# Cross-covariance attention on one core: every hand-off between engines one unit later

## The chip, the cores and the metric

The kernel runs on one core of one Trainium2 chip. The metric is the device time of one execution in microseconds. TensorE (PE) multiplies, VectorE (DVE) and ScalarE (ACT) work on elements, GpSimd (POOL) computes one small power here, and SyncE (SP) issues all transfers. Each engine takes its instructions strictly in the order in which they were written, and semaphores make it wait for the others. "PEld" in the profile is the loading of TensorE's weights.

## The reference

Q, K and V are 8 x 12 x 512 x 64 in float32: 96 heads of 512 rows and 64 columns. The attention is between columns, not rows.

```python
Q_norm = Q / (np.linalg.norm(Q, axis=-2, keepdims=True) + 1e-10)
K_norm = K / (np.linalg.norm(K, axis=-2, keepdims=True) + 1e-10)
attn = np.einsum('bhnd,bhne->bhde', Q_norm, K_norm)
attn = np.exp(attn - np.max(attn, axis=-1, keepdims=True))
attn = attn / (np.sum(attn, axis=-1, keepdims=True) + 1e-10)
return np.einsum('bhnd,bhde->bhne', V, attn).astype(np.float32)
```

## The kernel before

The 96 heads are worked in 24 units (U = 24) of four heads. For one unit the steps are, with the names that stand in the code and in the profile:

- **load_qk, load_v** (SyncE, L72, L73, L77): Q, K and V of the unit, 0.524 MB each, into buffers qf, kf, vf. Each has five buffers, so the load of unit u waits until unit u−5 has been cast.
- **casts** (VectorE, L85 to L88): Q and K of each head side by side in bf16, qkb. Before, the same function also casts V to vb (L90).
- **grams** (TensorE, L98): 16 matmuls of qkb with itself, so that one product holds QᵀQ, QᵀK and KᵀK (gram, two buffers in PSUM).
- **norms** (VectorE, L106): four masked sums over the diagonals of gram give the squared column norms nsq; GpSimd raises them to the power −0.5 (rq, L111).
- **scale_k** (VectorE, L117): the QᵀK blocks times the norms of K, kqs. It is the last reader of gram.
- **logits** (TensorE, L125): turns kqs into place, lg (one buffer in PSUM).
- **exps** (ScalarE, L131): exp with the norm of Q as its scale and the row sum beside it.
- **normalise** (VectorE, L137, L140): division by the sum, at in bf16.
- **doubled** (TensorE L146, then two ScalarE copies, L148 and L149): two copies of at, dup, then spread over a block-diagonal buffer ab (three of them, used in turn).
- **vtrans** (TensorE L156, then a ScalarE copy L158): eight transposes of vb, vps, then vt.
- **outs** (TensorE L168, then two ScalarE copies L172): V times the attention, 32 small matmuls, po, then so in float32 (ten buffers).
- **store** (SyncE, L80): 0.524 MB of output.

Nothing reorders these instructions: the order on each engine is that of the program text, in the loop over the steps s. In step s, the kernel before works on grams, norms, vtrans and scale_k of unit s, on logits, exps, normalise and doubled of unit s−1, on outs of unit s−2 and the casts of unit s+1. SyncE's queue holds, in this order, the loads of unit s+3 and the store of unit s−6, and is as strictly in order as the engines. Waits follow from the buffers: a step that writes a buffer waits until the last reader of its former content is done.

Of the kernel before, what the change touches and what calls it, by code (L numbers as in the profile page):

```python
# [25 lines left out]
def kernel(  # L26
# [11 lines left out]
    U = BH // HU  # L38
# [22 lines left out]
    ps_o = ctx.enter_context(tc.tile_pool(name="ps_o", bufs=2, space=bass.MemoryType.PSUM))  # L61

    LOAD_AHEAD = 3
    CAST_AHEAD = 1
    STORE_LAG = 6

# [2 lines left out]
    def load_qk(u):  # L69
        qf[u] = qp.tile([128, HU, T, D], F32, name="qf")  # L70
        kf[u] = qp.tile([128, HU, T, D], F32, name="kf")
        nc.sync.dma_start(out=qf[u], in_=Qf[:, u * HU:(u + 1) * HU])  # L72
        nc.sync.dma_start(out=kf[u], in_=Kf[:, u * HU:(u + 1) * HU])  # L73

    def load_v(u):
        vf[u] = vp.tile([128, SV, RV * D], F32, name="vf")
        nc.sync.dma_start(out=vf[u], in_=Vf[:, u * SV:(u + 1) * SV])  # L77

    def store(u):
        nc.sync.dma_start(out=Of[:, u * SV:(u + 1) * SV], in_=so[u])  # L80

    def casts(u):

        t_ = qkb[u] = qkp.tile([128, HU, T, 2 * D], BF16, name="qkb")
        nc.vector.tensor_copy(t_[:, 0::2, :, 0:D], qf[u][:, 0::2])  # L85
        nc.vector.tensor_copy(t_[:, 1::2, :, D:2 * D], qf[u][:, 1::2])  # L86
        nc.vector.tensor_copy(t_[:, 0::2, :, D:2 * D], kf[u][:, 0::2])  # L87
        nc.vector.tensor_copy(t_[:, 1::2, :, 0:D], kf[u][:, 1::2])  # L88
        w = vb[u] = vbp.tile([128, SV, TP, 2 * D], BF16, name="vb")
        nc.vector.tensor_copy(w.rearrange("p s t d -> p s (t d)"), vf[u])  # L90

    def grams(u):
        g = gram[u] = ps_g.tile([128, PU, 4, D], F32, name="gram")
        for h in range(HU):
            o = g[:, h // 2, 2 * (h % 2):2 * (h % 2) + 2, :]
            for t in range(T):
                x = qkb[u][:, h, t, :]
                nc.tensor.matmul(o, x, x, start=(t == 0), stop=(t == T - 1))  # L98

    def norms(u):  # L100

        n2 = nsq[u] = small.tile([128, 2, PU], F32, name="nsq")
        for p in range(PU):
            for c, (blk, m) in enumerate(((gram[u][:, p, 0::3, :], mask_q), (gram[u][:, p, 1:3, :], mask_k))):
                scr = small.tile([128, 2, D], F32, name="scr")
                nc.vector.tensor_tensor_reduce(  # L106
                    out=scr, in0=blk, in1=m, scale=1.0, scalar=1e-20,
                    op0=ALU.mult, op1=ALU.add, accum_out=n2[:, c, p:p + 1],
                )
        r = rq[u] = small.tile([128, 2, PU], F32, name="rq")  # L110
        nc.gpsimd.tensor_tensor(out=r, in0=n2, in1=mhalf, op=ALU.pow)  # L111

    def scale_k(u):

        kk = kqs[u] = small.tile([128, PU, 2, D], F32, name="kqs")
        for p in range(PU):
            nc.vector.scalar_tensor_tensor(  # L117
                out=kk[:, p], in0=gram[u][:, p, 0::3, :], scalar=rq[u][:, 1, p:p + 1], in1=off_diag,
                op0=ALU.mult, op1=ALU.mult,
            )  # L120

    def logits(u):
        l = lg[u] = ps_l.tile([128, PU, D], F32, name="lg")
        for p in range(PU):
            nc.tensor.matmul(l[:, p, :], kqs[u][:, p].rearrange("p a d -> p (a d)"), eye2)  # L125

    def exps(u):
        e = ex[u] = small.tile([128, PU, D], F32, name="ex")
        s = small.tile([128, PU], F32, name="esum")
        for p in range(PU):  # L130
            nc.scalar.activation(e[:, p, :], lg[u][:, p, :], AF.Exp, scale=rq[u][:, 0, p:p + 1], accum_out=s[:, p:p + 1])  # L131
        ex[u] = (e, s)

    def normalise(u):
        e, s = ex[u]
        ri = small.tile([128, PU], F32, name="rinv")
        nc.vector.reciprocal(ri, s)  # L137
        a = at[u] = small.tile([128, PU, D], BF16, name="at")
        for p in range(PU):
            nc.vector.tensor_scalar_mul(a[:, p, :], e[:, p, :], ri[:, p:p + 1])  # L140

    def doubled(u):

        d = ps_d.tile([128, 2, PU, D], F32, name="dup")
        for c in range(2):
            nc.tensor.matmul(d[:, c], pick[:, c, :], at[u])  # L146
        a = ab[u] = abuf[u % len(abuf)]
        nc.scalar.copy(a[0:D, :, :, 0, :], d[0:D].rearrange("p c u d -> p u c d"))  # L148
        nc.scalar.copy(a[D:, :, :, 1, :], d[D:].rearrange("p c u d -> p u c d"))  # L149

    def vtrans(u):

        ps = ps_v.tile([128, SV, TP, 128], BF16, name="vps")
        for g in range(SV):
            for t in range(TP):
                nc.tensor.transpose(ps[:, g, t, :], vb[u][:, g, t, :], identb)  # L156
        w = vt[u] = vtp.tile([128, SV, TP, 128], BF16, name="vt")
        nc.scalar.copy(w, ps)  # L158

    def outs(u):  # L160
        s = so[u] = sop.tile([128, SV, TP, 2 * D], F32, name="so")
        for i in range(2):
            po = ps_o.tile([128, 4, 2 * D], F32, name="po")
            for k in range(4):
                g, t = divmod(4 * i + k, TP)
                for x in range(HS):
                    h = g * HS + x
                    nc.tensor.matmul(  # L168
                        po[NV * x:NV * (x + 1), k, :], vt[u][:, g, t, NV * x:NV * (x + 1)],
                        ab[u][:, h // 2, h % 2].rearrange("p a d -> p (a d)"), tile_position=(0, NV * x),  # L170
                    )
            nc.scalar.copy(s.rearrange("p g t d -> p (g t) d")[:, 4 * i:4 * i + 4, :], po)  # L172


    for u in range(LOAD_AHEAD):
        load_qk(u)
        load_v(u)

    ident = const.tile([128, 128], F32, name="ident")
    make_identity(nc, ident)  # L180
# [24 lines left out]

    for u in range(CAST_AHEAD):
        casts(u)
    for s in range(U + 2):
        if s + LOAD_AHEAD < U:
            load_qk(s + LOAD_AHEAD)  # L210
            load_v(s + LOAD_AHEAD)
        if 0 <= s - STORE_LAG:
            store(s - STORE_LAG)
        if 0 <= s - 1 < U:
            logits(s - 1)
            exps(s - 1)
        if s < U:
            grams(s)
            norms(s)
            vtrans(s)  # L220
        if s + CAST_AHEAD < U:
            casts(s + CAST_AHEAD)
        if 0 <= s - 1 < U:
            normalise(s - 1)
        if s < U:
            scale_k(s)
        if 0 <= s - 2 < U:
            outs(s - 2)
        if 0 <= s - 1 < U:
            doubled(s - 1)  # L230
    for u in range(U + 2 - STORE_LAG, U):
        store(u)


# [28 lines left out]
```

## Time and profile before

| | us |
|---|---|
| median of 3 runs (167.81 to 170.22) | 169.07 |
| the profiled execution | 170.53 |
| its span, first to last instruction | 168.4 |
| PE busy | 105.2 (62%) |
| DVE busy | 94.6 (56%) |
| ACT busy | 83.4 (50%) |
| POOL busy | 33.7 (20%) |

The granted TensorE clock was 0.742 of full speed on average. In the groups and timelines of the profile a line gives the engine, the operation, what it writes and reads ("gram<-qkb"), the count, the busy time and the mean of one; in brackets or behind a bar stand the idle time ahead of it and what ended it. The chain of work is followed back from the last instruction. Buffer numbers are left out in the profile.

### The profile page before, as it was taken

To read this page: it belongs to the slowest core of one execution; us is meant where nothing else is said; L and a number is where in the kernel's file an instruction comes from. 1 tells how busy PE (TensorE), PEld (TensorE's weight loads), DVE (VectorE), ACT (ScalarE), POOL (GpSimd) and SP (SyncE) were. 2 spreads that over 40 slices of the span, in tenths; PEclk is the share of its full clock that TensorE was granted. 3 is DMA by queue.
4 is the path that set the end of the run, shared out by engine and by line. 5 is a ranking of instruction groups with operands and counts; after the bars stand their busy time and mean duration, and the time that the engine had idled before them with its cause. 6 is when DMAs were issued, how large, how long until landed. Compare 5 with 4: busy or idle time off the path is not lost.

```text
span 168.4 us, 4020 instructions
## 1 busy us (share of the span) xinstructions
PE 105.2 (62%) x1488; PEld 92.0 (55%) x1488; DVE 94.6 (56%) x432; ACT 83.4 (50%) x217; POOL 33.7 (20%) x45
## 2 busy tenths in 40 slices
PE   0427376494595667495595558486496687696860
PEld 0317275394484456385494457376385476495740
DVE  0573844836746863935845963844945853935410
ACT  3021354446437473546447483645555644446561
POOL 8220320302202220211202220220220220311200
PEclk9999996968769696967858796967858555555555
DMA  5999999999999999999999999999999303023053
GB/s 181 300 381 367 367 366 367 366 366 367 380 392 385 395 396 390 389 392 396 374 354 362 301 343 376 377 305 345 309 294 410 131 33 128 30 96 128 0 242 131
DMA packets 32274, 50.58 MB, mean 300 GB/s; under 512 B 1536, under 2 KB 26112, under 8 KB 32256
## 3 DMA queue, kind: packets, MB, share of 16 engines
q1 hardware_dynamic: 32256, 50.34, 85.2%
q8 instruction: 11, 0.18, 0.4%
q14 instruction: 7, 0.06, 0.1%
HBM read 37.75 MB, written 12.58 MB: 299 GB/s over the span
## 4 chain that ended last, share of the span: by engine, by line
DVE 46%; PE 40%; DMA 6%; issue 3%; SPq 1%; ACT 1%; POOLq 1%; ACTq 0%; DVEq 0%
PE gram L98 22%; PE lg L125 13%; DVE scr L106 12%; DVE vb L90 8%; DVE at L140 6%; DMA vf<-in_V_dram 6%; DVE qkb L85 4%; PE dup L146 4%; DVE qkb L87 4%; DVE qkb L88 4%; DVE qkb L86 4%; DVE rinv L137 1%; POOLq L258 1%; SPq L73 1%; SPq L72 1%
## 5 line engine op out<-in xcount | busy, mean ns | idle before, releaser
L111 POOL TENSOR_TENSOR rq<-nsq,mhalf 128x4 f32<-128x4 f32 x24 | 29.4, 1226 | 124.3 <-DVE nsq L106 118.8
L158 ACT COPY vt<-vps 128x1024 bf16<-128x1024 bf16 x24 | 24.3, 1012 | 46.1 <-PE vps L156 46.1
L98 PE MATMUL gram<-qkb 128*128 128x128 bf16 x384 | 43.1, 301 | 6.2 <-DVE qkb L87 6.2
L106 DVE CUSTOM_DVE_ANT_0 scr<-gram,ident 128x128 f32<-128x128 f32 x48 | 13.9, 289 | 56.3 <-PE gram L98 56.3
L98 PEld LDWEIGHTS <-qkb 128*128 128x128 bf16 x384 | 41.1, 148 | 6.2 <-DVE qkb L87 6.2
L146 PE MATMUL dup<-at,pick 128*128 128x128 bf16 x48 | 7.8, 253 | 45.7 <-DVE at L140 45.7
L146 PEld LDWEIGHTS <-pick 128*128 128x128 bf16 x48 | 3.0, 102 | 50.5 <-DVE at L140 47.7
L172 ACT COPY so<-po 128x512 f32<-128x512 f32 x48 | 25.9, 598 | 0.7 <-PE po L168 0.7
L125 PE MATMUL lg<-eye,kqs 128*128 128x64 f32 x96 | 22.6, 381 | 5.0 <-DVE kqs L117 4.1
L156 PE MATMUL vps<-identb,vb 128*128 128x128 bf16 x192 | 23.4, 297 | 1.1 <-DVE vb L90 1.1
L125 PEld LDWEIGHTS lg<-eye,kqs 128*128 128x128 f32 x96 | 19.0, 278 | 9.1 <-issue 4.5
L156 PEld LDWEIGHTS <-vb 128*128 128x128 bf16 x192 | 20.1, 144 | 1.4 <-DVE vb L90 1.4
L148 ACT CAST ab<-dup 64x256 bf16<-64x256 f32 x24 | 8.8, 366 | 24.3 <-PE dup L146 24.3
L168 PE MATMUL po<-ab,vt 128*32 128x128 bf16 x768 | 19.6, 261 | 0.9 <-ACT ab L149 0.9
L131 ACT ACTIVATE ex<-lg,rq 128x64 f32<-128x64 f32 x48 | 14.6, 309 | 9.2 <-PE lg L125 8.8
L90 DVE CAST vb<-vf 128x1024 bf16<-128x1024 f32 x24 | 16.4, 684 | 2.6 <-DMA vf<-in_V_dram 2.6
L168 PEld LDWEIGHTS <-vt 128*32 128x32 bf16 x768 | 14.6, 117 | 4.7 <-issue 3.6
L117 DVE SCALAR_TENSOR_TENSOR kqs<-gram,rq,off_diag 128x128 f32<-128x128 f32 x48 | 14.5, 344 | 0.7 <-POOL rq L111 0.7
L106 DVE CUSTOM_DVE_ANT_0 scr<-gram,swap 128x128 f32<-128x128 f32 x48 | 13.7, 286 | 0.0
L85 DVE CAST qkb<-qf 128x512 bf16<-128x512 f32 x24 | 10.8, 452 | 4.2 <-DMA qf<-in_Q_dram 4.2
L140 DVE TENSOR_SCALAR at<-ex,rinv 128x64 bf16<-128x64 f32 x48 | 10.0, 252 | 0.8
L87 DVE CAST qkb<-kf 128x512 bf16<-128x512 f32 x24 | 10.0, 418 | 0.7 <-DMA kf<-in_K_dram 0.7
(23 smaller groups left out, 56.1 us busy)
## 6 DMA issues: line engine op xcount, KB each, us to landing
qf<-in_Q_dram SPq DMA_DIRECT2D x24, 512.0 KB, 9.4
kf<-in_K_dram SPq DMA_DIRECT2D x24, 512.0 KB, 10.3
vf<-in_V_dram SPq DMA_DIRECT2D x24, 512.0 KB, 10.2
out_dram<-so SPq DMA_DIRECT2D x24, 512.0 KB, 8.3
```

What stands on the lines that cost most here:

```text
L85: nc.vector.tensor_copy(t_[:, 0::2, :, 0:D], qf[u][:, 0::2])
L90: nc.vector.tensor_copy(w.rearrange("p s t d -> p s (t d)"), vf[u])
L98: nc.tensor.matmul(o, x, x, start=(t == 0), stop=(t == T - 1))
L106: nc.vector.tensor_tensor_reduce(out=scr, in0=blk, in1=m, scale=1.0, scalar=1e-20, op0=ALU.mult, op1=ALU.add, accum_out=n2[:, c, p:p + 1],)
L111: nc.gpsimd.tensor_tensor(out=r, in0=n2, in1=mhalf, op=ALU.pow)
L125: nc.tensor.matmul(l[:, p, :], kqs[u][:, p].rearrange("p a d -> p (a d)"), eye2)
L140: nc.vector.tensor_scalar_mul(a[:, p, :], e[:, p, :], ri[:, p:p + 1])
L146: nc.tensor.matmul(d[:, c], pick[:, c, :], at[u])
L156: nc.tensor.transpose(ps[:, g, t, :], vb[u][:, g, t, :], identb)
L158: nc.scalar.copy(w, ps)
L168: nc.tensor.matmul(po[NV * x:NV * (x + 1), k, :], vt[u][:, g, t, NV * x:NV * (x + 1)], ab[u][:, h // 2, h % 2].rearrange("p a d -> p (a d) ...
L172: nc.scalar.copy(s.rearrange("p g t d -> p (g t) d")[:, 4 * i:4 * i + 4, :], po)
```

## The change

The loop over steps is written in another order, and the later stages of a unit move to later steps. Scale_k and logits of a unit come one step after its grams, as does its exps; normalise, doubled and vtrans two steps after; outs three. The cast of V is a function of its own, cast_v, one step after the grams and two after the casts of Q and K. Loads of V go out two steps later than those of Q and K of the same unit. The store's lag of six steps stays, so that it now comes three steps after outs and not four. There are U + 3 steps and not U + 2. What each function computes, its tiles and the number of buffers are as before.

```diff
     LOAD_AHEAD = 3
+    V_AHEAD = LOAD_AHEAD - 2
...
+    def cast_v(u):
         w = vb[u] = vbp.tile([128, SV, TP, 2 * D], BF16, name="vb")
         nc.vector.tensor_copy(w.rearrange("p s t d -> p s (t d)"), vf[u])
...
     for u in range(LOAD_AHEAD):
         load_qk(u)
-        load_v(u)
+        if u - 2 >= 0:
+            load_v(u - 2)
...
-    for s in range(U + 2):
-        if s + LOAD_AHEAD < U:
-            load_qk(s + LOAD_AHEAD)
-            load_v(s + LOAD_AHEAD)
-        if 0 <= s - STORE_LAG:
-            store(s - STORE_LAG)
-        if 0 <= s - 1 < U:
-            logits(s - 1)
-            exps(s - 1)
-        if s < U:
-            grams(s)
-            norms(s)
-            vtrans(s)
-        if s + CAST_AHEAD < U:
-            casts(s + CAST_AHEAD)
-        if 0 <= s - 1 < U:
-            normalise(s - 1)
-        if s < U:
-            scale_k(s)
-        if 0 <= s - 2 < U:
-            outs(s - 2)
-        if 0 <= s - 1 < U:
-            doubled(s - 1)
-    for u in range(U + 2 - STORE_LAG, U):
+    def on(f, u):
+        if 0 <= u < U:
+            f(u)
+    for s in range(U + 3):
+        on(load_qk, s + LOAD_AHEAD)
+        on(load_v, s + V_AHEAD)
+        on(store, s - STORE_LAG)
+        on(casts, s + CAST_AHEAD)
+        on(scale_k, s - 1)
+        on(normalise, s - 2)
+        on(grams, s)
+        on(norms, s)
+        on(cast_v, s - 1)
+        on(vtrans, s - 2)
+        on(outs, s - 3)
+        on(logits, s - 1)
+        on(doubled, s - 2)
+        on(exps, s - 1)
+    for u in range(U + 3 - STORE_LAG, U):
         store(u)
```

VectorE before, from the end of the norms of unit 2 to the first norms instruction of unit 3. A number behind a name tells buffers apart; gram_290 is the product of unit 2, gram_399 that of unit 3:

```order
L106 ISA nsq_307 128x1
L85 CAST qkb_329<-qf_150 128x2x4x64
L86 CAST qkb_329<-qf_150 128x2x4x64
L87 CAST qkb_329<-kf_151 128x2x4x64
L88 CAST qkb_329<-kf_151 128x2x4x64
L90 CAST vb_334<-vf_154 128x1024
L137 RECIPROCAL rinv_336<-esum_287 128x2
L140 TENSOR_SCALAR at_338<-ex_286,rinv_336 128x64 x2
L117 SCALAR_TENSOR_TENSOR kqs_341<-gram_290,rq_316,off_diag_126 128x128 x2
L106 ISA scr_417,nsq_416<-gram_399,ident_114 128x128
```

VectorE after the change, the step of unit 3 with its neighbours; gram_253 is the product of unit 2, gram_325 that of unit 3 (line numbers here are those of the changed kernel, one to three higher for the same work):

```order
L93 CAST vb_281<-vf_148 128x1024
L86 CAST qkb_312<-qf_183 128x2x4x64
L87 CAST qkb_312<-qf_183 128x2x4x64
L88 CAST qkb_312<-kf_184 128x2x4x64
L89 CAST qkb_312<-kf_184 128x2x4x64
L120 SCALAR_TENSOR_TENSOR kqs_317<-gram_253,rq_279,off_diag_122 128x128 x2
L140 RECIPROCAL rinv_320<-esum_303 128x2
L143 TENSOR_SCALAR at_322<-ex_302,rinv_320 128x64 x2
L109 ISA scr_343,nsq_342<-gram_325,ident_110 128x128
L109 ISA nsq_342 128x1
```

The norms of a unit stood ahead of its own scale_k with the casts, the cast of V and normalise between them; now scale_k and normalise of older units stand ahead of the norms, and the cast of V behind them.

TensorE before, where one step's outs end and the next step begins:

```order
L168 MATMUL po_472<-ab1_137,vt_255 32x128
L146 LDWEIGHTS pick_130
L146 MATMUL dup_490<-at_447,pick_130 128x128
L146 LDWEIGHTS pick_130
L146 MATMUL dup_490<-at_447,pick_130 128x128
L125 MATMUL lg_501<-eye2_124,kqs_450 128x64 x2
L98 LDWEIGHTS qkb_438
L98 MATMUL gram_508<-qkb_438 128x128
```

TensorE after, at the same place:

```order
L171 MATMUL po_494<-ab1_133,vt_364 32x128
L128 MATMUL lg_512<-eye2_120,kqs_426 128x64 x2
L149 LDWEIGHTS pick_126
L149 MATMUL dup_515<-at_431,pick_126 128x128
L149 LDWEIGHTS pick_126
L149 MATMUL dup_515<-at_431,pick_126 128x128
L101 LDWEIGHTS qkb_421
L101 MATMUL gram_543<-qkb_421 128x128
```

Dup, then lg, stood between the outs of a step and the grams of the next, and dup read what VectorE's normalise had written in the same step. Now lg stands ahead of dup, both at the end of a step, and dup belongs to an older unit than lg.

SyncE after the change, in the middle of the run (before, each row of vf stood with the Q and K of its own unit):

```order
L73 DMA qf_743<-in_Q_dram 128x4x256
L74 DMA kf_744<-in_K_dram 128x4x256
L78 DMA vf_747<-in_V_dram 128x1024
L81 DMA out_0_dram<-so_475 128x1024
L73 DMA qf_853<-in_Q_dram 128x4x256
```

The counts in a row are as before: three loads and one store; the V among them is two units older.

## The prediction

> **What bounds the kernel now.** I first read the chain of work that ended last.
>
> ```profile
> DVE 46%; PE 40%; DMA 6%; issue 3%; SPq 1%; ACT 1%; POOLq 1%; ACTq 0%; DVEq 0%
> ```
>
> 86% of the span is VectorE and TensorE taking turns, and transfers are 6%. The same chain in order of time (start, duration, what) shows one turn, with the first dup on it ahead:
>
> ```profile
> 20.11 0.37 PE dup L146 x2
> ...
> 146.79 0.40 PE dup L146 x2
> 147.18 1.04 PE lg L125 x4
> 148.22 1.72 PE gram L98 x16
> 149.94 0.02 issue
> 149.97 0.29 DVE scr L106
> ...
> 150.90 0.34 DVE qkb L85
> ...
> 152.24 0.60 DVE vb L90
> ...
> 153.43 0.39 PE dup L146 x2
> ```
>
> From dup to dup it is 153.43 − 146.79 = 6.64 us (21 turns from 20.11 on take 6.35 on average), and each piece starts when the one before it ends: TensorE 3.16 us (dup, lg, gram), then VectorE 3.41 us (norms 0.93, the four casts 1.34, vb 0.60, rinv and at 0.54). That is a serial loop. The list of waits says the same of the whole run (total us, times, longest):
>
> ```profile
> DVE scr L106 <- PE gram L98: 56.3, 23, 2.7
> PEld L146 <- DVE at L140: 47.7, 23, 2.7
> ```
>
> So neither engine is full. Their loads per unit come from the windows (busy PE, PEld, DVE, ACT, POOL, then granted clock, DMA share, GB/s):
>
> ```profile
> 0.00:10.00 10.00, 2.69 (x24) 2.40 (x24) 3.76 (x14) 1.28 (x1) 4.26 (x21) 1.00 0.84 264
> 20.00:40.00 20.00, 13.01 (x186) 11.63 (x185) 11.74 (x56) 10.27 (x27) 3.82 (x3) 0.83 1.08 366
> 50.00:75.00 25.00, 16.46 (x271) 14.34 (x272) 15.96 (x79) 13.77 (x37) 4.85 (x4) 0.78 1.06 391
> 90.00:125.00 35.00, 23.53 (x340) 20.84 (x340) 21.03 (x101) 18.54 (x51) 6.07 (x5) 0.77 1.02 336
> 133.50:153.43 19.93, 14.90 (x187) 12.96 (x187) 11.67 (x55) 10.27 (x27) 3.88 (x3) 0.50 0.20 80
> sum 168.40, PE 105.24 PEld 92.05 DVE 94.64 ACT 83.39 POOL 33.68; mean PE 6.19 PEld 5.41 DVE 5.57 ACT 4.91 POOL 1.98
> ```
>
> VectorE: 94.64 / 24 = 3.94 us per unit; ScalarE: 83.39 / 24 = 3.47. TensorE depends on the clock, which the timeline of PE shows in two steps:
>
> ```profile
> 58.92 0.28 PE L146 MATMUL dup<-at,pick 128*128 128x128 bf16 x2 [1.67 <-DVE at L140]
> 61.17 0.63 PE L168 MATMUL po<-ab,vt 128*32 128x128 bf16 x32
> 64.29 0.38 PE L146 MATMUL dup<-at,pick 128*128 128x128 bf16 x2 [2.50 <-DVE at L140]
> 146.79 0.40 PE L146 MATMUL dup<-at,pick 128*128 128x128 bf16 x2 [1.67 <-DVE at L140]
> 150.71 1.04 PE L168 MATMUL po<-ab,vt 128*32 128x128 bf16 x32
> ```
>
> At the slow clock a unit's matmuls take 150.71 + 1.04 − 146.79 = 4.96 us, at the fast one 61.17 + 0.63 − 58.92 = 2.88 us.
>
> Last, the transfers: SyncE's timeline and the page's count of bytes.
>
> ```profile
> 59.40 2.41 SPq L77 DMA_DIRECT2D vf<-in_V_dram  x1
> 90.37 0.38 SPq L80 DMA_DIRECT2D out_dram<-so  x1
> 94.57 0.38 SPq L72 DMA_DIRECT2D qf<-in_Q_dram  x1
> HBM read 37.75 MB, written 12.58 MB: 299 GB/s over the span
> ```
>
> Up to 75 us the V issue (59.40) takes 2.41 us where the other two take 0.38: the ring is full, and 366 GB/s (reads alone) and 391 (reads and stores) are what the queue gives when it is fed. Later SyncE waits for buffers (nothing is issued from 90.75 to 94.57), and the rate is the demand: 2.097 MB per unit / 6.35 us = 330, close to the 336 measured. The DMA share stays above 1 there, so it doesn't tell a saturated queue from a fed one. Four transfers of 0.524 MB per unit at 391 GB/s take **5.36 us per unit**.
>
> **The change, part by part.** *The loop goes.* Now logits(s−1) and doubled(s−2) stand behind grams(s), vtrans(s−2) and outs(s−3) on TensorE; on VectorE scale_k(s−1) and normalise(s−2) work on what the last step left, ahead of norms(s). The norms of a unit and the grams of the next no longer wait for each other in turn. What remains per unit is the largest of VectorE 3.94, ScalarE 3.47, TensorE 2.88 to 4.96, and transfers 5.36 us. No instruction is added or taken away.
>
> *Waits inside a step.* Two scale_k of a unit take 0.60 us:
>
> ```profile
> 146.64 0.60 DVE L117 SCALAR_TENSOR_TENSOR kqs<-gram,rq,off_diag 128x128 f32<-128x128 f32 x2
> ```
>
> Let casts(s+1) start at T. scale_k ends at T + 1.34 + 0.60 = T + 1.94, normalise at T + 2.5, norms(s) at T + 3.4, cast_v(s−1) at T + 4.0. TensorE at the slow clock begins lg at T + 1.94, then dup, grams, transposes and outs: it is back at lg at T + 1.94 + 4.96 = T + 6.90, and the next scale_k ends at T + 5.36 + 1.94 = T + 7.30. So it has 0.4 us to spare even there, 2.4 at the fast clock. scale_k(s) needs the GpSimd power, whose row is
>
> ```profile
> L111 POOL TENSOR_TENSOR rq<-nsq,mhalf 128x4 f32<-128x4 f32 x24 | 29.4, 1226 | 124.3 <-DVE nsq L106 118.8 <-DVE rinv L137 5.4
> ```
>
> 1.23 us after norms; cast_v (0.60) and the next casts (1.34) run meanwhile, 1.94 us: I cost it at nothing. Without that cover it is 1.3 us per step on VectorE, 3.94 + 1.3 = 5.2, still under 5.36. ScalarE's exps(s−1) come last in the step and are wanted by normalise a step later, over 3 us of room.
>
> *A new wait: casts come first.* When a load is late, VectorE stops at casts(s+1) with scale_k, normalise, norms and cast_v behind it, and TensorE's lg and dup behind those. This is how the transfers set the pace; it costs nothing beyond their 5.36.
>
> *SyncE.* At its step s it waits for casts(s−2), cast_v(s−4) and outs(s−6), which all fall in compute step s−3 now (outs fell in s−4). It so issues qk(s+3) at about compute step s−2, wanted in step s+2: 4 steps, 21 us, for a load that the page lands 9.4 to 10.3 us after issue:
>
> ```profile
> qf<-in_Q_dram SPq DMA_DIRECT2D x24, 512.0 KB, 9.4
> kf<-in_K_dram SPq DMA_DIRECT2D x24, 512.0 KB, 10.3
> ```
>
> The queue stays fed. The later V loads bring qk(1) and qk(2) 1.4 and 2.9 us (0.524 and 1.049 MB at 366) nearer at the start; that is hidden by the pace of transfers, so nothing.
>
> *The sum.* Start: 10 us moved 2.64 MB, which is 7.2 us at 366, so 2.8 us are lost. Before the first store stand Q and K of 10 units and V of 8, 14.68 MB: 40.1 us at 366, to 42.9. Q and K of unit 23 are preceded by V 0–20 and stores 0–13: 43.52 MB, so 28.84 MB more at 391 = 73.8 us, **landed at 116.7**. All 50.33 MB would be through at 42.9 + 35.65 / 0.391 = 134.1.
>
> The drain of unit 23: casts 1.34, the rest of that step 2.7 (120.7); in the next step scale_k(22) waits for its power (to 121.3), then 0.60 + 0.54 + 0.93 to norms(23) at 123.4; power 1.23, 124.6. From there the old tail gives the price:
>
> ```profile
> 158.81 0.36 DVE kqs L117
> ...
> 163.85 0.58 ACT so L172
> 164.44 0.49 ACTq L258
> ```
>
> The last ScalarE copy ends at 164.93, so 6.1 us from scale_k: 130.7. vtrans(23) and outs(22) now stand ahead of doubled(23) on TensorE, 2.1 us of which some 1.1 show, and ScalarE's copies for them about 0.7, both estimates from the rows of po (1.04) and of the copies: 132.5. From there to the span's end it was 168.4 − 164.93 = 3.5 us: **136.0**. The transfers' own end, 134.1, lies just inside. The profiled execution took 170.53 us for a span of 168.4, so 2.1 more: 138.1. The median shown, 169.07, is 1.5 below that execution; I take **138 us** and leave the rest for frictions.
>
> **Rivals.**
> *A: TensorE sets the pace at the slow clock.* If the clock stays at 0.50, as from 133.5 us on, and hand-offs cost 0.6 to 0.9 us per step beside the 4.96, the step is 5.6 to 5.9 us. From the dup at 20.11 to that at 153.43 before has 21 steps of 6.35; the saving would be 21 × 0.45 to 0.75 = 9 to 16 us: span 152 to 159, time **154 to 161**. For it: that clock with PE busy 75% of the time. Against it: the 0.4 us to spare worked out above. 0.13.
> The page TensorE: Matmul & The Clock Gate of the Trainium skill (Part 1) says that sustained activity of about 3.4 us gives the full clock, and an idle window of that length takes it away. By that rule a TensorE with shorter gaps would run at full clock and A would fall; the trace agrees only in part, since gaps of 1.67 us held 0.50 for 20 us.
>
> *B: the queue gives less under denser engines.* The rate fell to 336 where demand fell; part of that may have been contention. With 366 or 336 GB/s instead of 391 after the first 42.9 us, Q and K of unit 23 land at 121.7 or 128.7; with 19.3 us of drain and 2.1 around the span that is **143 to 150**. Against it: 391 over 25 us with both directions in use. 0.08.
> The page HBM Reference of the Trainium skill (Specifications) gives about 358 GB/s as a core's effective share, at which 50.33 MB alone take 140.6 us, an estimate. The trace disagrees, with its 366 and 391, and the same section says that a core streaming alone gets more than the share.
>
> *C: nothing moves.* Another loop of the same length closes (through two gram buffers, say, or one lg buffer). gram(s) is freed a step later by scale_k(s), a step ahead of grams(s+2), so I see none. **167 to 171**. 0.04.
>
> *D: slower.* SyncE's in-order queue runs dry. The store of outs(s−6), one unit later now, holds back the loads behind it; VectorE's first instruction waits for those, and all older units with it, which makes outs later still. A two-microsecond window of before shows a dry queue:
>
> ```profile
> 92.00:94.00 2.00, 2.00 (x33) 0.50 0.98 263
> ```
>
> At 263 GB/s the bytes take 191.4 us, and with 2.8 at the start and 2.1 around the span the time is **196**. It decides when the mean rate falls under 50.33 MB / 165 us = 305 GB/s. Against it: 21 us of lead for 10 us of landing. 0.05.
>
> **How the numbers follow.** Forecast (133 to 143, the rate between about 380 and 400): 0.70. With B and the low end of what A may give, to 152, the range holds 8 in 10: 133 to 152. Faster by over 2%: forecast, A and B, 0.91; within 2% (about what a measurement tells, the runs shown reach from 167.81 to 170.22): C, 0.04; slower: D, 0.05.
>
> **What would show it.** Right: dup-to-dup about 5.4 us; GB/s flat near 390 from 45 to 120 us; VectorE's L86 casts waiting for qf or kf; V issues that take over 2 us to the end; a chain in which DMA, not PE and DVE in turn, has the largest share; qk(23) landing near 117 and the last store issued near 132. Wrong: the rate at 336 with SyncE waiting on ACT so (D); casts that never wait while PE has no gaps at clock 0.50 (A); scr still waiting 2.7 us for gram each step (C).

## The result, and the profile after

The changed kernel takes 141.16 us (median of 4 runs, 140.67 to 141.53) against 169.64 (4 runs, 167.81 to 170.56): 0.835 of the time before, 95% interval 0.827 to 0.843. Some executions of one and the same kernel take some per cent longer than its fastest, and two of those below took far longer (218.02 us of the changed kernel, 165.47 of the one whose stores lag twelve steps), so every ratio here is taken over the fast executions alone and can differ from the quotient of two medians. The profiled execution of the changed kernel took 140.83 us, with a span of 138.7. The forecast was 138, with 133 to 152 as its range.

The shares of the chain that ended last, by engine, changed hands:

```profile
DMA 76%; DVE 8%; SPq 5%; ACT 3%; PE 3%; issue 1%; POOL 1%; ACTq 0%; POOLq 0%
```

In order of time it is now one K load after another (L73 and L74 are Q and K):

```profile
98.38 10.38 DMA kf<-in_K_dram
...
108.78 0.13 DVE qkb L88
108.91 10.38 DMA kf<-in_K_dram
...
119.31 0.43 DVE qkb L88
```

A load lands and its cast starts at once. The step from a cast to the next load 0.13 us later is not a wait, though the chain is drawn so: the load at 98.38 is that of unit 21, and its buffer was free since the casts of unit 16 at about 82 us. What it waited for is seen on SyncE, which issues one transfer right after another:

```profile
97.26 1.02 SPq L73 DMA_DIRECT2D qf<-in_Q_dram  x1
98.38 1.77 SPq L74 DMA_DIRECT2D kf<-in_K_dram  x1
```

The Q ahead of it was issued until 98.28, and the load then needed 10.38 us to land. From 98.38 to 108.91 are two units, 5.27 us each. At 119.31 the K of the last unit is cast. The waits agree: VectorE's casts, which hardly waited before, wait for loads nearly every step, and TensorE's lg waits behind them.

```profile
PE lg L128 <- DVE kqs L120: 24.0, 18, 2.6
DVE qkb L86 <- DMA qf<-in_Q_dram: 16.7, 16, 4.3
DVE qkb L88 <- DMA kf<-in_K_dram: 14.0, 23, 1.5
```

The windows (busy PE, PEld, DVE, ACT, POOL, granted clock, DMA share, GB/s) and one V issue on SyncE:

```profile
20.00:30.00 10.00, 8.51 (x146) 7.47 (x146) 9.27 (x46) 7.79 (x23) 3.37 (x3) 1.00 1.07 368
70.00:80.00 10.00, 6.83 (x122) 5.84 (x120) 7.72 (x36) 6.59 (x17) 2.54 (x3) 0.84 1.06 393
100.00:110.00 10.00, 8.77 (x124) 8.00 (x123) 7.46 (x35) 6.23 (x17) 3.07 (x2) 0.57 1.06 392
sum 138.70, PE 89.97 PEld 77.31 DVE 95.73 ACT 82.92 POOL 38.31; mean PE 6.43 PEld 5.52 DVE 6.84 ACT 5.92 POOL 2.74
```

```profile
100.24 2.38 SPq L78 DMA_DIRECT2D vf<-in_V_dram  x1
```

The rate is flat: 366 to 369 GB/s from 10 to 40 us, while only reads run, and 392 to 399 with stores, from 50 us up to the drain at 120. V issues still take over 2 us at 100 us, as they did before the change only in the stretch in which the queue was fed. VectorE and ScalarE are busy as long as before in total (95.73 and 82.92 us). TensorE's 15 us less of busy time, for the same 1488 matmuls, go with its clock, 0.842 on average for 0.742. In the window from 100 to 110 us the clock fell to 0.57, TensorE was busy 88% of the time, and the rate stayed at 392: the clock does not set the pace.

### The profile page after: what moved, and what is told of

Read it like the earlier page. It is cut to its first block, busy times and chain, and to the rows that moved or that the text cites. A ratio compares the mean times of both kernels' runs of the same rounds, so it can differ in the third digit from the quotient of the medians.

```text
span 138.7 us, 4018 instructions
## 1 busy us (share of the span) xinstructions
PE 90.0 (65%) x1488; PEld 77.3 (56%) x1488; DVE 95.7 (69%) x432; ACT 82.9 (60%) x217; POOL 38.3 (28%) x45
## 4 chain that ended last, share of the span: by engine, by line
DMA 76%; DVE 8%; SPq 5%; ACT 3%; PE 3%; issue 1%; POOL 1%; ACTq 0%; POOLq 0%
DMA kf<-in_K_dram 76%; SPq L73 2%; DVE scr L109 2%; SPq L74 2%; DVE qkb L88 2%; DVE kqs L120 2%; DVE at L143 1%; PE po L171 1%; ACT so L175 1%; SPq L78 1%; POOL rq L114 1%; PE lg L128 1%; PE vps L159 1%; DVE qkb L89 1%; ACT vt L161 1%
## 5 line engine op out<-in xcount | busy, mean ns | idle before, releaser
L114 POOL TENSOR_TENSOR rq<-nsq,mhalf 128x4 f32<-128x4 f32 x24 | 34.1, 1419 | 87.8 <-DVE nsq L109 74.0
L101 PE MATMUL gram<-qkb 128*128 128x128 bf16 x384 | 35.0, 263 | 9.4 <-DVE qkb L88 9.4
L101 PEld LDWEIGHTS <-qkb 128*128 128x128 bf16 x384 | 31.4, 122 | 9.7 <-DVE qkb L88 9.7
L128 PE MATMUL lg<-eye,kqs 128*128 128x64 f32 x96 | 18.3, 323 | 28.0 <-DVE kqs L120 24.0
L128 PEld LDWEIGHTS lg<-eye,kqs 128*128 128x128 f32 x96 | 15.3, 227 | 32.0 <-ACT so L175 18.6
L159 PE MATMUL vps<-identb,vb 128*128 128x128 bf16 x192 | 20.0, 265 | 4.4 <-DVE vb L93 4.4
L88 DVE CAST qkb<-kf 128x512 bf16<-128x512 f32 x24 | 10.2, 427 | 14.1 <-DMA kf<-in_K_dram 14.0
L159 PEld LDWEIGHTS <-vb 128*128 128x128 bf16 x192 | 15.8, 123 | 6.7 <-DVE vb L93 6.6
L171 PE MATMUL po<-ab,vt 128*32 128x128 bf16 x768 | 18.0, 247 | 1.5 <-ACT ab L152 1.5
L93 DVE CAST vb<-vf 128x1024 bf16<-128x1024 f32 x24 | 16.5, 689 | 0.0
L171 PEld LDWEIGHTS <-vt 128*32 128x32 bf16 x768 | 13.5, 110 | 5.0 <-issue 3.4
L89 DVE CAST qkb<-kf 128x512 bf16<-128x512 f32 x24 | 10.1, 420 | 0.0
## 6 DMA issues: line engine op xcount, KB each, us to landing
kf<-in_K_dram SPq DMA_DIRECT2D x24, 512.0 KB, 10.4
```

What stands on the lines that cost most here:

```text
L171: nc.tensor.matmul(po[NV * x:NV * (x + 1), k, :], vt[u][:, g, t, NV * x:NV * (x + 1)], ab[u][:, h // 2, h % 2].rearrange("p a d -> p (a d) ...
```

## The experiments

The theory is that a serial loop through TensorE and VectorE set 6.35 us per unit, that the later hand-offs open it, and that the transfers then set the pace. Three questions follow. Is it the distance in units that does it, and of which hand-off? Were the transfers no bound before, and are they the bound now? How much would the TensorE clock have given alone?

### One later hand-off instead of three

The loop over steps of the changed kernel, with attention and outputs a unit earlier. Before, lg of a unit stood just ahead of the grams of the next unit; here, as in the changed kernel, scale_k is a step later and lg stands behind those grams. The casts also stay ahead of the norms.

```diff
-    for s in range(U + 3):
+    for s in range(U + 2):
...
         on(scale_k, s - 1)
-        on(normalise, s - 2)
         on(grams, s)
+        on(logits, s - 1)
+        on(exps, s - 1)
         on(norms, s)
-        on(cast_v, s - 1)
-        on(vtrans, s - 2)
-        on(outs, s - 3)
-        on(logits, s - 1)
-        on(doubled, s - 2)
-        on(exps, s - 1)
+        on(cast_v, s)
+        on(normalise, s - 1)
+        on(vtrans, s - 1)
+        on(outs, s - 2)
+        on(doubled, s - 1)
```

> Only scale_k and logits stay one unit later; normalise, doubled and vtrans come one step earlier than in the changed kernel (unit s-1), outs in step s-2, the cast of V in the step of its grams; VectorE's order is casts(s+1), scale_k(s-1), norms(s), cast_v(s), normalise(s-1). Theory (one later hand-off, that of the logits, opens the loop; transfers then set 5.36 us per unit): the longest loop left is grams 1.72, norms 0.93, cast_v 0.60, normalise 0.54, dup 0.4, together 4.2 us and under 5.36, so 139 to 143 us, 0.97 to 1.02 of the changed kernel. Rival (every hand-off has to be one unit later): dup waits for VectorE again each step and the time goes back at least half the way, 150 us or more.

Measured: 142.59 us (141.69 to 143.65), 0.837 of the kernel before (0.829 to 0.845), where the whole change has 0.835 (0.827 to 0.843). TensorE's dup does wait for VectorE again,

```profile
PEld L149 <- DVE at L143: 30.2, 22, 2.5
DVE vb L93 <- DMA vf<-in_V_dram: 24.6, 20, 2.7
```

30.2 us in total, and it costs nothing that can be measured, since VectorE waits for loads of V in the same steps. That is a balance of two shifts: the last K is cast at 122.7 us and not at 119.3, but with one step less at the end the span closes 16.6 us later and not 19.4. So the later hand-off of the logits, with the casts in their new place, is enough; the later attention and outputs bring no measurable time. The hand-off without the new place of the casts was not run.

### The order inside a step, without any distance

First only normalise is moved ahead of the norms of the next unit, in the kernel before:

```diff
             logits(s - 1)
             exps(s - 1)
+            normalise(s - 1)
...
-        if 0 <= s - 1 < U:
-            normalise(s - 1)
```

> The kernel before with one edit: normalise(s-1) is written ahead of norms(s) and not behind the casts; no hand-off is later. Theory: dup no longer waits at the end of the step, but scale_k(s) still stands behind norms(s) and the casts, and logits(s) wait for it: scale_k 0.36, lg 1.1, gram 1.72, norms 0.93, casts and vb 1.94, 0.15 between, 6.2 us at the slow clock against 6.64: 158 to 164 us. Rival (the loop was that of dup alone): 140 to 147 us.

Measured: 153.16 us, 0.896 (0.887 to 0.905), 5 us under what the theory said and 6 over the rival. The timeline of PE shows lg from step to step:

```profile
63.70 1.08 PE L125 MATMUL lg<-eye,kqs 128*128 128x64 f32 x4 [1.17 <-ACT ab L148]
69.81 0.63 PE L125 MATMUL lg<-eye,kqs 128*128 128x64 f32 x4 [1.63 <-ACT ab L148]
75.09 0.63 PE L125 MATMUL lg<-eye,kqs 128*128 128x64 f32 x4 [1.30 <-DVE kqs L117]
...
119.77 0.63 PE L125 MATMUL lg<-eye,kqs 128*128 128x64 f32 x4 [1.17 <-ACT ab L148]
```

The slow step is 6.11 us, near the 6.2 worked out, but with the full clock it is 5.28, and the ten steps from 63.70 to 119.77 take 5.61 on average. The expectation had priced the slow clock alone. (Where a line names the ab copy of ScalarE, scale_k's first product ended at about the same time: it ran from 63.21 for 0.34 us.) In a fast step the chain does not go through the grams either:

```profile
85.78 0.64 PE lg L125 x4
...
86.51 0.71 ACT ex L131 x4
...
87.44 0.42 DVE at L140 x2
87.86 0.20 DVE scr L106
...
90.65 0.27 DVE kqs L117
...
91.06 0.82 PE lg L125 x4
```

From lg to lg it is 91.06 − 85.78 = 5.28 us, through exps and normalise, behind which the norms now stand. So the loop through scale_k, lg and the grams was there at the slow clock, as described, and at the full clock a second loop through exps sets the step, which the expectation had left out.

Then VectorE's order is brought near to that of the changed kernel, again with no hand-off later: normalise, casts, norms, cast of V, scale_k.

```diff
             exps(s - 1)
+            normalise(s - 1)
+        if s + CAST_AHEAD < U:
+            casts(s + CAST_AHEAD)
         if s < U:
             grams(s)
             norms(s)
             vtrans(s)
         if s + CAST_AHEAD < U:
-            casts(s + CAST_AHEAD)
-        if 0 <= s - 1 < U:
-            normalise(s - 1)
+            cast_v(s + CAST_AHEAD)
```

> No hand-off is later than before, but VectorE's order is near that of the changed kernel: normalise(s-1), casts(s+1), norms(s), cast of V, scale_k(s). Theory (the distance in units matters, not the order inside a step): scale_k 0.36, lg 1.1, exps 0.8, normalise 0.6, casts 1.34, norms 0.93, power 1.3 close a loop of 6.5 us: 163 to 172 us, no gain. Rival (the order of VectorE's work makes the gain): 140 to 150 us.

Measured: 176.49 us, 1.037 (1.028 to 1.045): slower than before, a little above the expected 163 to 172. The chain goes around the loop that was named, with the GpSimd power now in it:

```profile
78.84 1.31 POOL rq L113
...
80.17 0.36 DVE kqs L119
...
80.67 0.64 PE lg L127 x4
...
81.39 0.71 ACT ex L133 x4
...
82.75 0.34 DVE qkb L85
...
85.10 1.31 POOL rq L113
```

85.10 − 78.84 = 6.26 us in a fast step. So an order much like the new one, without the later hand-off, is worse than the old one. Order alone is not without effect, though: moving only normalise took 10.4% off the time, well over half of the 16.5% that the whole change takes off. Neither of the two orders reached the time of the changed kernel; other orders were not run.

### Are the transfers the bound, before and after?

Both kernels without the V loads of units 5 to 23, 9.96 of the 50.33 MB:

```diff
     def load_v(u):
+        if u >= 5:
+            vf[u] = vf[u % 5]
+            return
         vf[u] = vp.tile([128, SV, RV * D], F32, name="vf")
```

> The kernel before without the V loads of units 5 to 23: the first five V buffers are read again, so the output is that of other V; 9.96 of 50.33 MB are not moved. Theory (before, transfers do not bound it): 166 to 171 us, no change. Rival (transfers bound both kernels): 20% less, about 135 to 145 us.

> The changed kernel without the V loads of units 5 to 23, as above. Theory (transfers set its pace): three transfers per unit are 4.02 us, so the engines become the limit: VectorE 3.94 us per unit of busy time, TensorE 2.9 to 5.0 by its clock; 4.2 to 5.0 us per unit, 114 to 130 us. Rival (the engines already set 5.4 us per unit): 138 to 142 us.

Measured: for the kernel before, a median of 170.48 us against 170.2 with all loads, ratio 1.020 (1.005 to 1.035), so nothing was gained by a fifth less traffic. The changed kernel falls to 120.38 us, ratio 0.724 (0.710 to 0.737). A window of it:

```profile
50.00:100.00 50.00, 37.20 (x782) 30.26 (x771) 48.41 (x228) 42.96 (x111) 16.38 (x13) 1.00 1.07 391
```

The rate is the same 391 GB/s with three transfers per unit instead of four, and VectorE is busy 48.41 of 50 us. The chain meets the K casts of units that are nine apart at 61.51 and 97.80, 4.03 us per unit:

```profile
61.51 0.43 DVE qkb L91
...
97.80 0.43 DVE qkb L91
```

So the engines of the changed kernel can do a unit in about 4.0 us, and transfers and VectorE are equal there. Both halves of the theory hold.

### The clock alone

In the kernel before, 16 matmuls whose product nobody reads are put where TensorE waits for normalise:

```diff
+    def filler(u):
+        for _ in range(FILL):   # FILL = 16
+            nc.tensor.matmul(l_full[u][:, 4:6, :], identb, identb)
...
         if 0 <= s - 1 < U:
+            filler(s - 1)
             doubled(s - 1)
```

> The kernel before with 16 additional matmuls of 128x128 per step, ahead of dup, where TensorE waits 1.7 us for VectorE; their product is read by nothing. Theory A (the granted clock follows how densely TensorE is fed): the clock rises from 0.74 to 0.9 or more, the step falls from 6.35 to about 5.4 us, 145 to 152 us. Theory B (the clock does not follow that): the clock stays, time 168 to 176 us. If A holds, a good part of the gain of the change could be had through the clock alone, without a later hand-off.

Measured: 152.72 us, 0.908 with a wide interval (0.874 to 0.942). The granted clock was 0.887 to 0.926 in its four runs, and 0.703 to 0.838 in those of the kernel before beside it. A turn of the old loop:

```profile
81.59 0.30 PE dup L153 x2
...
81.94 0.63 PE lg L128 x4
82.57 0.91 PE gram L100 x16
...
86.97 0.30 PE dup L153 x2
```

5.38 us in place of 6.64, and as long as a turn of the kernel before at the full clock (from the dup at 58.92 to that at 64.29, 5.37 us). So it is the clock that shortened it. That is as long as the transfers of a unit, yet the kernel is some 11 us slower than the changed one. The casts of K show where the difference lies (minimum, median and maximum duration, then first and last start), first with the filler, then of the changed kernel:

```profile
L89 DVE CAST qkb<-kf x24: 415/418/427, 5.8 to 135.8; 128x512 bf16<-128x512 f32 x24
```

```profile
L88 DVE CAST qkb<-kf x24: 426/427/428, 5.8 to 119.3; 128x512 bf16<-128x512 f32 x24
```

(135.8 − 5.8) / 23 = 5.65 us per unit against 4.93. While only reads run, a unit's three loads need 1.573 MB at 368, 4.3 us. The loop can't use that, the changed kernel can; two of its dups there are 4.2 us apart, and when it casts the K of unit 9, at 44.77 us, it is already 12 us ahead:

```profile
24.24 0.29 PE L149 MATMUL dup<-at,pick 128*128 128x128 bf16 x2
28.45 0.28 PE L149 MATMUL dup<-at,pick 128*128 128x128 bf16 x2
```

So a good part of the gain could be had by feeding TensorE more densely, but not all.

### The V loads

The changed kernel with V loaded together with Q and K:

```diff
-    V_AHEAD = LOAD_AHEAD - 2
+    V_AHEAD = LOAD_AHEAD
...
         load_qk(u)
-        if u - 2 >= 0:
-            load_v(u - 2)
+        load_v(u)
```

> The changed kernel, but V is loaded with Q and K of its unit, three steps ahead, its cast still one step after the grams, with the five V buffers as they are. Theory: the load of V(s+3) then waits for cast_v(s-2) of compute step s-1, and Q and K of the next step stand behind it on SyncE: they go out about two steps before they are wanted, 10.7 us for 9.5 to 10.4 us of landing, so the queue runs dry at times: 144 to 155 us. Rival (the trailing V loads do nothing): 140 to 142 us. Rival (they are the main part): over 160 us.

Measured: 143.84 us (143.74 to 144.02), 0.844 (0.837 to 0.851), just under what was expected and for another reason. The rate did not sag: 392 to 394 GB/s from 60 to 120 us. The last K is cast later:

```profile
122.06 0.43 DVE qkb L88
```

at 122.06 and not 119.31, 2.75 us. Two more V loads stand ahead of the last Q and K, 1.049 MB, and at 391 GB/s those are 2.7 us. By the trace the trailing V loads are thus worth some 2 to 3 us at the end; V is wanted last in the drain, so nothing is lost by loading it behind. The ratios alone don't settle it, as this interval overlaps that of the changed kernel (0.827 to 0.843). That the queue would run dry was wrong.

### The end

The same thought with the stores: a lag of nine steps puts three more of them behind the last loads.

```diff
-    STORE_LAG = 6
+    STORE_LAG = 9
```

> The changed kernel with the stores nine steps behind and not six. Theory (transfers set the pace up to Q and K of the last unit, then 15.9 us of drain follow): three stores less stand ahead of those loads, 3 x 1.34 = 4.0 us, less 0.8 us for a longer stretch of reads alone at 366 GB/s; all bytes through by 134, so the end moves by 1 to 3 us: 138 to 140 us. Rival (the stores at the end are the bound): 141 us or more.

Measured: 139.3 us, ratio 0.835 (0.829 to 0.842), so against the kernel before on its own chip no gain over the changed kernel shows. By the traces, K of the last unit is cast at 116.3 us and not at 119.3, but the span is only 1.7 us shorter, 137.0: the last store, issued at 132.3, is done 4.7 us later, where it took 3.4 in the changed kernel (issued at 135.3). Three variants and the changed kernel again were then run on one chip. They have 16 output buffers (`sop`), lags of nine and twelve, and in one the vt copies of the last three units are on VectorE:

```diff
-        nc.scalar.copy(w, ps)
+        if u < U - 3:
+            nc.scalar.copy(w, ps)
+        else:
+            nc.vector.tensor_copy(w, ps)
```

> The changed kernel itself once more, beside the three variants of its end, so that they can be compared on one chip: 140 to 142 us.

> Stores nine steps behind and 16 output buffers in place of 10 (with 10, ScalarE's copy waited for a store at 122.3 us). Theory (with a lag of nine the end is set by the transfers themselves, which moved over 400 GB/s up to 130 us): no more than 0.5 us under the 139.3 of ten buffers, 138.5 to 139.5 us, 0.98 to 0.99 of the changed kernel. Rival (the wait for an output buffer sets the end): 136 to 138 us.

> Stores twelve steps behind, 16 output buffers. Theory: Q and K of the last unit come another 3 us sooner, but the transfers are the end already, and three more units are read at 366 and not at 391 GB/s: 139 to 141 us, no better than nine steps. Rival (the drain is the end): 135 to 137 us.

> As the kernel with a lag of nine and 16 buffers, and the copies of vps to vt of the last three units are made by VectorE, since ScalarE is busy 99% of the time from 125 to 130 us. Theory (transfers are the end): under 1 us better, 138 to 139.5 us. Rival (ScalarE's drain is the end): three copies of 1.01 us less, 135.5 to 137 us.

Measured, on that chip: changed kernel 141.0 us, ratio 0.836 (0.830 to 0.842); lag nine with 16 buffers 139.67, just over the 138.5 to 139.5 expected, 0.830 (0.825 to 0.835); lag twelve 140.62, 0.834 (0.829 to 0.839); lag nine with VectorE's copies **138.88 us**, 0.827 (0.821 to 0.832). With lag twelve the stores were issued by 128.4 and none landed in under 8.4 us:

```profile
L81 SPq DMA_DIRECT2D out_dram<-so x24: 332/338/1107, 63.4 to 128.4; - x24
DMA to landing us min/median/max: 8.4/9.8/11.0
```

The queue is full to the end there, and the rate stands at 408 to 419 GB/s from 110 to 130 us: with a lag of twelve the transfers alone are the time. ScalarE's copies are worth some 0.8 us by the medians (139.67 to 138.88), with runs that overlap; the 16 buffers brought nothing that shows, though with 10 they ran on another chip (139.3). The fastest version is 1.5% under the changed kernel on the same chip. Each of its six runs (138.62 to 139.88) is shorter than each of the changed kernel's (140.28 and more), but the intervals of the two ratios just overlap, so that it beats the changed kernel is likely rather than certain.

## Why the prediction was right

- **The loop goes.** Right: an order near the new one without the distance is slower than before (1.037), and the distance for the logits alone, with the casts ahead of the norms, gives the whole gain (0.837). The prediction held the three distances to work together; two of them are not needed for the time.
- **5.36 us per unit from the transfers.** Measured 5.27, with 392 to 399 GB/s for 391. Without a fifth of the traffic the changed kernel goes to 120.38 us and the kernel before stays.
- **Waits inside a step at nothing.** Right: in a step at the slow clock TensorE has 0.43 us to spare, where the prediction had worked out 0.4:

```profile
104.68 1.08 PE L128 MATMUL lg<-eye,kqs 128*128 128x64 f32 x4 [0.43 <-DVE kqs L120]
```

- **Q and K of the last unit land at 116.7.** They were cast from 117.9 on, K at 119.3, 2.6 us late, and that is nearly the whole error of the forecast (138 for 141.16). The mis-sized term: the prediction let the bytes arrive strictly in the order of issue, 43.52 MB by then. Summed over the windows up to 119.3 us, 44.8 MB had moved, of which at most 0.24 MB are instructions. So 1.0 to 1.3 MB of later transfers, 2.6 to 3.3 us of them at 393 GB/s, went alongside the last loads. A sum of the bytes ahead of these loads came out too early by about that.
- **The drain.** Predicted 15.8 us from the landing to the last ScalarE copy, measured 15.9 (119.31 to 135.23). The size is right, the path is not, so that the two agree is in part luck: I had followed scale_k, lg, exps, normalise, dup with 1.8 us for work in between. In the chain the end is ScalarE, which goes from the copies of one unit straight to those of the next, with one stop for TensorE's last outs:

```profile
129.46 0.37 ACT ab L151
...
130.93 0.90 ACT vt L161
131.84 0.25 ACT so L175
...
133.49 0.64 PE po L171 x16
...
134.16 0.58 ACT so L175
134.74 0.49 ACTq L259
```

- **After the last copy, and around the span.** 3.5 and 2.1 us were predicted; 138.7 − 135.23 = 3.5 and 140.83 − 138.7 = 2.1 measured.
- **V trailing.** The prediction called it nothing at the start, and there the rate was 366 to 369 GB/s from 10 us on. Its worth at the end was in the sum without being named: V 0 to 20 and not V 0 to 22 stand ahead of the last Q and K, two loads, 2.7 us at 391 GB/s. With V loaded together with Q and K the last K came 2.75 us later.
- **Rivals.** A (TensorE at the slow clock): at 0.57, from 100 to 110 us, the pace held, so it fell. The full clock came at about 23 us, some 4 us after TensorE's last gap, which ended at 19.25: the 16 grams took 1.91 us at 20.35 and 1.06 from 24.36 on. The page TensorE: Matmul & The Clock Gate of the Trainium skill (Part 1) says that about 3.4 us of sustained activity give the full clock, and that it falls after an idle window of that length. The trace agrees with the first; with the second it does not, since from 40 to 120 us the clock was 0.57 to 0.86 though lg never waited longer than 2.6 us. B: the rate was 392 to 399 from 50 to 120 us with VectorE busy 69% of the span and not 56%; it fell. C: the order without the later hand-off (176.49 us) shows that such a loop exists, but not in this change; it fell. D: the rate stayed flat, and but for one wait of 0.3 us SyncE waited for outputs only after 113 us, when the last Q and K had been issued; it fell.

## What to carry to other kernels

Where two engines with strictly ordered instructions are each half busy and each waits for the other once per unit, draw the loop and look for the one hand-off whose distance of one unit opens it; moving instructions inside the step can shorten the loop, as normalise did, or close a longer one. Then ask what is next: here it was in the trace already, in the stretches where SyncE's issues took over 2 us. Once transfers set the pace, what is wanted last in the drain should also stand last in the queue.

## What the runs showed of the hardware

- The TensorE clock could be raised from outside: 16 matmuls per step that nobody reads, in a gap of 1.7 us, took it from 0.742 to 0.926 and cut a turn of the loop from 6.64 to 5.38 us. The work added made the kernel about 9% faster.
- The granted clock in the windows is 1.00 for the first 20 us of both kernels, but the matmuls run at the slow pace there: the 16 grams of a unit took 1.89 to 1.91 us, and 1.06 later at the full clock. The averages 0.742 and 0.842 hold this stretch as full clock.
- A DMA share of 1.0 to 1.1 does not show a saturated queue: it stood at 1.02 for 336 GB/s before and 1.06 for 392 after. The time of a V issue on SyncE told the two apart, over 2 us when the queue was fed and 0.34 us in the sparsest steps before.
- Towards the end, as stores outweigh reads, the rate rises further. With a lag of nine, from 120 to 125 us:

```profile
120.00:125.00 5.00, 4.33 (x92) 3.60 (x91) 3.31 (x17) 3.87 (x13) 1.73 (x2) 0.80 1.03 417
```

- GpSimd's power of four values per partition took 1.42 us on average after the change, 1.23 before, with the same operands. No run asked why:

```profile
L114 POOL TENSOR_TENSOR rq<-nsq,mhalf 128x4 f32<-128x4 f32 x24 | 34.1, 1419 | 87.8 <-DVE nsq L109 74.0
```
